# First layer: the gated rows of seven heads turned by VectorE in 32x32 blocks and through DRAM, the norm's weight applied where they are split

## The chip, the cores and the metric

The kernel runs on one core of a Trainium2 chip. The metric is device time in microseconds of one execution; times shown are medians of several runs. One more execution is taken with the hardware profiler, and all lines of the profile come from that one.

## What is computed

A decoder of two layers on 512 rows of 2048 columns, in float32. The first layer has differential attention with 8 heads (two score maps of 128 columns each, values of 256 columns); the second has another attention with 16 heads, which the change does not touch. Of the reference, cut to the first layer's part behind the attention weights:

```python
def rms_norm(x, g):
    xf = x.astype(jnp.float32)
    y = xf * lax.rsqrt(jnp.mean(jnp.square(xf), axis=-1, keepdims=True) + EPS)
    return (y * g.astype(jnp.float32)).astype(x.dtype)

def diff_attention(h, w_in, w_out, lq1, lk1, lq2, lk2, subln_g, layer_idx):
    ...
        a = p[:, :, 0] - lam * p[:, :, 1]
        return jnp.einsum('bhqk,bkhe->bqhe', a.astype(v.dtype), v)

    o = from_blocks(lax.map(block, (to_blocks(q), jnp.arange(S // BLOCK))))
    o = rms_norm(o, subln_g) * (1.0 - lam_init)
    o = o.reshape(B, S, A_WIDTH) * jax.nn.silu(g)
    return o @ w_out
```

So each head gives 512 rows of 256 columns `o`, which are normalised over their 256 columns, multiplied by the norm's weight `subln_g` (one number per column, the same for all heads), gated, and multiplied with `w_out`.

## The kernel before

TensorE (PE) multiplies in a format of fewer bits than float32, so each float32 operand is cut into a high part (a cast on ScalarE, ACT) and the remainder (a subtraction on VectorE, DVE); `split` does that, and `products` (lines 212 to 214) makes three matmuls of each product: high times high, high times low, low times high. [...]

The weights stream through four buffers `wst` of 512 KB, one per block of 256 weight rows, loaded by SyncE (SP) three blocks ahead; ACT and DVE cut each block into `whi` and `wlo` (lines 117 and 118) two blocks ahead of PE. `group` runs one set of 512 weight columns: 8 blocks, each with four bursts of six matmuls. After every burst it calls `tick`, which takes the next entry of the list `pieces` (an entry is a function, a list of functions, or nothing) and now and then a step of `background`, the sums of the modulation weights (`ms`, `macc`, line 440) that DVE makes. In this way the attention of one head is written, step by step, between the bursts of another head's projection. `drain` empties the list.

The groups run in this order: the rest of heads 0 and 1, the query and key columns of head 2 with head 0's attention beside them, the value and gate columns of head 2 with head 1's attention, and then for h = 3 to 7 the query and key columns of head h and the value and gate columns of head h with the attention of head h - 1 spread over both. Head 7's attention stands in the first group of the output projection, which follows.

`attention_a(h)` makes one head's steps. `score(i, comp)` makes a 128-row block of one score map and its exponentials in a tile `e` (four buffers). The weights of row block i must be transposed before they can be multiplied with the values. In heads 0, 1 and 7 (`turn`) PE does that through the PSUM bank `tr`, which has one buffer. In heads 2 to 6 (`spread`) `turn_small` lets DVE transpose 32x32 blocks, writes the result to DRAM (`turned`), `send` reads it back in four DMAs that put the blocks in place, and `take` cuts it into `ah` and `al` (lines 790 and 791). `values(i)` multiplies with the values; after every second i, `norm(p)` makes the gated rows `og` of two row blocks, p = 0 or 1 (128 partitions, 2 row blocks, 256 columns; one buffer): two reads of the PSUM bank on ACT (816, 817), the reciprocal root in some ten short DVE instructions, and the gate (821).

The output projection needs the gated rows transposed, columns on partitions. `store(i)` does it for one row block: two PE transposes of 128x128 into the bank `tr` (line 835) and two ACT instructions (line 837) that move them to `ogT`, with the norm's weight `subg`, a column with one number per partition, as their scale. `ogT` has 16 tiles of 128x512, two per head (e = 0 and 1 for the two halves of the 256 columns), in the pool `K` of 16 buffers. In the last projection group (`vg[7]`), `split_og` cuts them into `Hh` and `Hl`, four instructions for each head's two tiles (lines 207 and 208 as called from line 884): heads 0 to 6 there, head 7 after its attention.

The order of each engine's instructions is that in which the steps are written, as the scheduler of the framework lays them down at build time. All loads, stores and turned blocks in this part are issued by SP, in one queue; an instruction that waits there holds what is behind it. The steps that the prediction speaks of are `store` (827 to 840), the lists that `attention_a` returns (842 to 857), `split_og` (881 to 884) and the lines that put the lists into `pieces` (887 to 920).

Of the kernel before, what the change touches and what calls it, by code (L numbers as in the profile page):

```python
# [148 lines left out]
def tile_yoco(  # L149
# [23 lines left out]
    nc = tc.nc  # L173
    V, S, PE, G = nc.vector, nc.scalar, nc.tensor, nc.gpsimd
# [8 lines left out]
    kpool = ctx.enter_context(tc.tile_pool(name="kpool", bufs=16))  # L183
    wpool = ctx.enter_context(tc.tile_pool(name="wpool", bufs=2))
    ps = ctx.enter_context(tc.tile_pool(name="ps", bufs=1, space=PSUM))
    dram = ctx.enter_context(tc.tile_pool(name="dram", bufs=1, space=bass.MemoryType.DRAM))
# [19 lines left out]
    def split(hi, lo, src):  # L206
        S.copy(hi, src)
        V.tensor_tensor(lo, src, hi.bitcast(F32), op=ALU.subtract)
# [114 lines left out]
    pieces = []  # L323
# [360 lines left out]
    def evac_qk(h):  # L684
        def fn(b, acc):
            name = ("q0", "q1", "k0", "k1")[b]
            hi = ap.tile([P, T], F32R, name=name + "h", tag=name + "h")
            lo = ap.tile([P, T], F32R, name=name + "l", tag=name + "l")
            if b < 2:
                S.activation(hi, acc, AF.Copy, scale=QS)  # L690
                V.scalar_tensor_tensor(lo, acc, QS, hi.bitcast(F32), op0=ALU.mult, op1=ALU.subtract)
            else:
                split(hi, lo, acc)
            cur[h, name] = (hi, lo)
        return fn
# [16 lines left out]
    def attention_a(h, lead=3, late=(), spread=False):  # L712
# [5 lines left out]
        def score(i, comp):  # L718
            def fn():
                if i == 0 and comp == 0:  # L720
                    bias = ap.tile([P, 512], F32, name="bias", tag="bias", bufs=1)
                    V.scalar_tensor_tensor(bias, dist, -slope, mask, op0=ALU.mult, op1=ALU.add)
                    st["bias"] = bias
                if comp == 0:
                    st["mn", i] = ap.tile([P, 2], F32, name="mn", tag="mn", bufs=2)
                    st["rs", i] = ap.tile([P, 2], F32, name="rsum", tag="rsum", bufs=2)
                w = (i + 1) * P
                n = max(w, 256)
                q, k = cur[h, f"q{comp}"], cur[h, f"k{comp}"]
                sc = sc_bank()  # L730
                ts = slice(i * P, (i + 1) * P)
                products(sc[:, :n], (q[0][:, ts], q[1][:, ts]), (k[0][:, :n], k[1][:, :n]), True, True)
                e = ap.tile([P, 512], F32, name="e", tag="e", bufs=4)
                mn, rs = st["mn", i][:, comp : comp + 1], st["rs", i][:, comp : comp + 1]
                V.tensor_tensor_reduce(  # L735
                    out=e[:, :w], in0=sc[:, :w], in1=st["bias"][:, (3 - i) * P :], scale=-1.0, scalar=3.0e38,
                    op0=ALU.add, op1=ALU.min, accum_out=mn,
                )
                S.activation(e[:, :w], e[:, :w], AF.Exp, bias=mn, scale=-1.0, accum_out=rs)  # L739
                st["e", i, comp] = e  # L740
                if comp == 1:
                    rs = st["rs", i]
                    r = ap.tile([P, 2], F32, name="rrec", tag="rrec", bufs=4)
                    V.reciprocal(r, rs)
                    V.scalar_tensor_tensor(r[:, 1:2], r[:, 1:2], neglam, rs[:, 0:1], op0=ALU.mult, op1=ALU.mult)
                    e0, e1 = st["e", i, 0], e
                    V.scalar_tensor_tensor(e0[:, :w], e1[:, :w], r[:, 1:2], e0[:, :w], op0=ALU.mult, op1=ALU.add)
                    st["r", i] = r[:, 0:1]
            return fn

        def turn(i):
            def fn():
                w = (i + 1) * P
# [41 lines left out]
        def values(i):  # L795
            def fn():
                if i % 2 == 0:
                    st["o", i // 2] = o_bank()
                o = st["o", i // 2][:, (i % 2) * 256 : (i % 2 + 1) * 256]
                ah, al = st["a", i]  # L800
                vh, vl = cur[h, "v"]
                for j in range(i + 1):
                    js = slice(j * P, (j + 1) * P)
                    products(o, (ah[:, js], al[:, js]), (vh[:, j, :], vl[:, j, :]), j == 0, j == i)
                if i % 2 == 1:
                    norm(i // 2)
            return fn
# [19 lines left out]
        def store(i):  # L827
            def fn():
                if i == 0:
                    for e in range(2):  # L830
                        ogT[2 * h + e] = kpool.tile([P, T], F32, name="ogT", tag="K")
                pt = tr_bank()
                og = st["og", i // 2]
                for e in range(2):
                    PE.transpose(pt[:, e * P : (e + 1) * P], og[:, i % 2, e * P : (e + 1) * P], ident)  # L835
                for e in range(2):
                    S.activation(
                        ogT[2 * h + e][:, i * P : (i + 1) * P], pt[:, e * P : (e + 1) * P], AF.Copy, scale=subg[:, e : e + 1]
                    )
            return fn  # L840

        if spread:
            r, d, k = ([part(i) for i in range(TB)] for part in (turn_small, send, take))
            first = [
                score(0, 0), None, score(0, 1), None, [score(1, 0), r[0]], None, [score(1, 1), d[0]], None, [k[0], r[1]], None,
                [score(2, 0), d[1]], values(0), k[1], None, score(2, 1), None, [values(1), r[2]], score(3, 0), d[2], None, k[2],
                score(3, 1),
            ]
            rest = [
                values(2), r[3], store(0), d[3], store(1), k[3], None, None, None, values(3), *[None] * 9, store(2), None, store(3),  # L850
            ]
            return first, rest
        return [
            *[None] * lead, score(0, 0), *late[0:1], score(0, 1), *late[1:2], score(1, 0), *late[2:3], score(1, 1), *late[3:4],
            turn(0), score(2, 0), values(0), turn(1), score(2, 1), values(1), score(3, 0), turn(2), score(3, 1), None,
            values(2), store(0), turn(3), store(1), values(3), None, None, None, None, store(2), store(3),
        ]

    def drain():
        while pieces:  # L860
# [20 lines left out]
    def split_og(kts):  # L881
        for kt in kts:
            new_h(kt)
            split(Hh[kt], Hl[kt], ogT[kt])


    drain()
    pieces.append(lambda_columns)
    pieces.extend(attention_a(0, 2))
    group(qk[2], False, lambda b, acc: keep(("qk", b), acc), bg=lambda k: k % 3 == 2)  # L890
    drain()
    pieces.extend(first_qk(1))
    pieces.append(lambda: evac_qk(1)(3, raw["k1"]))
    pieces.extend(attention_a(1, 2, first_vg(1, part[1])))

    def keep_vg(b, acc):
        if b == 0:
# [4 lines left out]
    for h in range(3, A_HEADS):  # L902

        first_steps, rest = attention_a(h - 1, spread=True)
        if h == 3:
            pieces.extend(lambda b=b: evac_qk(2)(b, raw["qk", b]) for b in range(4))
            late = first_vg(2, raw)
            for n in range(4):
                first_steps[2 * n + 1] = late[n]
        else:  # L910
            pieces.extend([None] * 4)
        pieces.extend(first_steps)

        def evac(b, acc, h=h):
            if b == 0:
                drain()
            evac_qk(h)(b, acc)

# [12 lines left out]
        group(vg[h], True, evac_rest, bg=lambda k: k % 8 in (1, 4, 6), after_sub=early if h == A_HEADS - 1 else None)  # L931
# [549 lines left out]
```

## Time and profile before

| | us |
|---|---|
| median of 3 runs (1960.11 to 1963.65) | 1962.01 |
| the profiled execution, whole | 1961.92 |
| its span, first to last instruction | 1960.1 |
| PE busy in it | 1930.6 |
| DVE busy | 1320.9 |
| ACT busy | 708.3 |

The span is cut by the profile into instructions with a start and a duration. A line such as L835 is that of kernel.py. PE's matmuls overlap each other, so that their durations add up to more than the time they take; their starts tell how many follow each other in a stretch. "PEld" is PE's loading of the stationary operand. A name like `tr<-ident,og` gives output and inputs by the program's tile names. The number behind "idle before" or in square brackets is how long the engine stood idle ahead of the instruction, and the arrow what ended it. "SPq" is SP's queue, in which DMAs are issued.

### The profile page before, as it was taken

Reading aid. Unit: us, or ns where it says so; the run is one execution under the profiler, and the core shown is the slowest. Engines: PE = TensorE matmul, PEld = TensorE weight load, DVE = VectorE, ACT = ScalarE, POOL = GpSimd, SP = SyncE. Lnnn points to the kernel's source line nnn. Section 1 sums busy time; section 2 is a strip of 40 time slices with the busy share of each in tenths; the row PEclk is TensorE's granted clock in tenths of the full one; section 3 lists DMA queues with packets and bytes.
Section 4 is the critical chain, followed back from the end, with each engine's and each line's share of the span. In section 5 each row is a group of like instructions: output and inputs, shape, how many; then the busy total and the mean of one; then the engine's idle time right before and its main releaser. Section 6 shows DMA issues by size and latency. Waiting matters only on the chain.

```text
span 1960.1 us, 25084 instructions
## 1 busy us (share of the span) xinstructions
PE 1930.6 (98%) x8861; PEld 1600.3 (82%) x8861; DVE 1320.9 (67%) x2316; ACT 708.3 (36%) x1233; POOL 2.2 (0%) x10
## 2 busy tenths in 40 slices
PE   7999999999999999999999999999999999999997
PEld 6788888888888888888888888888888888888886
DVE  7794678877777777553475665666466666696657
ACT  3322445333333334431264222224343444453123
POOL 0000000000000000000000000000000000000000
PEclk9999999999999999999999999999999999999999
DMA  9993465777777775262345765664355555556622
GB/s 351 346 328 97 152 196 176 245 225 237 227 238 234 237 228 181 86 170 97 114 155 195 262 231 194 222 222 136 103 152 154 153 158 147 156 160 217 203 88 106
DMA packets 301018, 371.40 MB, mean 189 GB/s; under 512 B 57526, under 2 KB 220620, under 8 KB 300124
## 3 DMA queue, kind: packets, MB, share of 16 engines
q1 hardware_dynamic: 298464, 365.56, 58.3%
q10 hardware_dynamic: 2428, 4.23, 0.6%
q8 instruction: 70, 1.15, 0.2%
q14 instruction: 56, 0.46, 0.1%
HBM read 343.27 MB, written 26.43 MB: 189 GB/s over the span
## 4 chain that ended last, share of the span: by engine, by line
PE 94%; DVE 3%; DMA 2%; ACT 1%; issue 0%; SPq 0%; DVEq 0%; ACTq 0%
PE acc L212 27%; PE acc L213 26%; PE acc L214 26%; PE acc L623 3%; PE sc L625 2%; DMA sms<-in_w_mod_dram 1%; PE o L212 1%; PE sc L214 1%; PE sc L213 1%; PE o L214 1%; PE sc L212 1%; PE o L213 1%; PE o L625 1%; DVE sacc L535 1%; PE tr L835 0%
## 5 line engine op out<-in xcount | busy, mean ns | idle before, releaser
L118 DVE TENSOR_TENSOR wlo<-wst,whi 128x1024 fp32r<-128x1024 f32 (+1 forms) x290 | 350.0, 1207 | 353.9 <-ACT whi L117 344.5
L117 ACT CAST whi<-wst 128x1024 fp32r<-128x1024 f32 (+1 forms) x290 | 301.1, 1039 | 634.0 <-PE acc L214 334.6
L212 PE MATMUL acc<-hh,whi 128*128 128x512 f32 x1184 | 463.9, 392 | 0.0
L213 PE MATMUL acc<-hl,whi 128*128 128x512 f32 x1184 | 461.8, 390 | 0.0
L214 PE MATMUL acc<-hh,wlo 128*128 128x512 f32 x1184 | 461.5, 390 | 0.0
L212 PE MATMUL acc<-whi,hh 128*128 128x512 f32 x1104 | 434.6, 394 | 0.0
L214 PE MATMUL acc<-whi,hl 128*128 128x512 f32 x1104 | 430.6, 390 | 0.0
L213 PE MATMUL acc<-wlo,hh 128*128 128x512 f32 x1104 | 430.5, 390 | 0.1
L214 PEld LDWEIGHTS acc<-hh,wlo 128*128 128x128 f32 x1184 | 222.3, 188 | 47.2
L212 PEld LDWEIGHTS acc<-hh,whi 128*128 128x128 f32 x1184 | 222.6, 188 | 42.8
L213 PEld LDWEIGHTS acc<-hl,whi 128*128 128x128 f32 x1184 | 222.6, 188 | 41.9
L214 PEld LDWEIGHTS acc<-whi,hl 128*128 128x128 f32 x1104 | 207.3, 188 | 43.9
L213 PEld LDWEIGHTS acc<-wlo,hh 128*128 128x128 f32 x1104 | 207.5, 188 | 40.9 <-DVE wlo L118 0.5
L212 PEld LDWEIGHTS acc<-whi,hh 128*128 128x128 f32 x1104 | 207.4, 188 | 40.8
L440 DVE SCALAR_TENSOR_TENSOR macc<-ms,cact,macc 128x1024 f32<-128x1024 f32 (+1 forms) x180 | 198.1, 1101 | 25.5 <-DMA ms<-in_kv_w_mod_dram 13.5
L535 DVE SCALAR_TENSOR_TENSOR sacc<-sms,cact,sacc 128x512 f32<-128x512 f32 x117 | 87.8, 751 | 12.2 <-DMA sms<-in_w_mod_dram 9.3
L739 ACT ACTIVATE e<-e,mn 128x128 f32<-128x128 f32 (+3 forms) x64 | 36.0, 563 | 100.7 <-DVE mn L735 97.6
L126 ACT CAST whi<-wst 128x768 fp32r<-128x768 f32 (+1 forms) x32 | 30.1, 942 | 113.4 <-DMA wst<-in_a_w_in_dram 46.5
L1283 ACT ACTIVATE eb<-eb,mnb 128x128 f32<-128x128 f32 (+1 forms) x64 | 36.0, 563 | 86.0 <-DVE mnb L1280 85.8
L623 PE MATMUL acc<-whi,hh 128*128 128x512 f32 x128 | 51.8, 409 | 0.0
L623 PE MATMUL acc<-wlo,hh 128*128 128x512 f32 x128 | 50.6, 395 | 1.2 <-DVE wlo L135 1.2
L623 PE MATMUL acc<-whi,hl 128*128 128x512 f32 x128 | 50.7, 396 | 0.0
(273 smaller groups left out, 1996.3 us busy)
## 6 DMA issues: line engine op xcount, KB each, us to landing
wst<-in_a_w_in_dram SPq DMA_DIRECT2D x240, 256.0 KB, 3.9
ms<-in_w_mod_dram SPq DMA_DIRECT2D x64, 512.0 KB, 4.3
ms<-in_kv_w_mod_dram SPq DMA_DIRECT2D x64, 512.0 KB, 4.5
wst<-in_kv_w_dram SPq DMA_DIRECT2D x64, 512.0 KB, 3.7
sms<-in_w_mod_dram SPq DMA_DIRECT2D x56, 512.0 KB, 7.5
wst<-in_b_w_in_dram SPq DMA_DIRECT2D x112, 256.0 KB, 3.0
wst<-in_a_w_out_dram SPq DMA_DIRECT2D x32, 512.0 KB, 3.6
msk<-in_w_mod_dram SPq DMA_DIRECT2D x64, 256.0 KB, 5.3
```

What stands on the lines that cost most here:

```text
L117: self.nc.scalar.copy(hi[:, :, :w], st[:, :, :w])
L118: self.nc.vector.tensor_tensor(lo[:, :, :w], st[:, :, :w], hi[:, :, :w].bitcast(F32), op=ALU.subtract)
L126: self.nc.scalar.copy(hi[:, :, : job.width], self.stage[self.done][:, :, : job.width])
L212: PE.matmul(dst, lhs[0], rhs[0], start=start, stop=False)
L213: PE.matmul(dst, lhs[0], rhs[1], start=False, stop=False)
L214: PE.matmul(dst, lhs[1], rhs[0], start=False, stop=stop)
L440: ins = V.scalar_tensor_tensor(acc, w, cact[:, kt : kt + 1], acc, op0=ALU.mult, op1=ALU.add)
L535: V.scalar_tensor_tensor(acc, w, sc, acc, op0=ALU.mult, op1=ALU.add)
L623: PE.matmul(bank(v, b), h[:, bs], w, start=start, stop=stop)
L625: PE.matmul(bank(v, b), w[:, bs], h, start=start, stop=stop)
L739: S.activation(e[:, :w], e[:, :w], AF.Exp, bias=mn, scale=-1.0, accum_out=rs)
L1283: S.activation(e[:, :w], e[:, :w], AF.Exp, bias=mn, scale=-1.0, accum_out=rs)
```

## The change

For heads 0 to 6 the PE transposes are left out. `turn_rows(p)` lets DVE transpose the 32x32 blocks of the gated rows of two row blocks into an `e` tile, writing every fourth column, and writes this to DRAM (256 KB, a contiguous run per partition). `send_rows(p)` reads it back in four DMAs of 64 KB, in runs of 512 bytes, into a tile `ogR` of the pool `K`. The result holds, for p, the columns of the head on partitions with the two halves e and the four row sets interleaved in the free dimension: position (t, r, e) is row t of row block 2p + r, half e. `split_og` takes it apart: for each of the two tiles `Hh`, `Hl` of a head it reads half a tile from each `ogR` with a step of four elements, and applies the weight `subg` there, as ACT's scale and in DVE's instruction, which now multiplies and subtracts. Per head that is four ACT and four DVE instructions of 128x256 instead of two and two of 128x512. Head 7 keeps `store`.

In the spread heads the first write stands where `store(0)` was, one step ahead of `send(3)`; its read follows three steps later, together with `take(3)`. The second write stands where `store(2)` was, and its read three steps later. In heads 0 and 1 the last two functions of a head are given back as `rows_left` and put beside the first steps of the next head (the evictions of its queries and keys).

```diff
+        def turn_rows(p):
+            def fn():
+                t = ap.tile([P, 512], F32, name="e", tag="e", bufs=4)
+                src = st["og", p].rearrange("p r (e b c) -> p b (r e) c", e=2, b=4)
+                V.transpose(t.rearrange("p (b m n) -> p b n m", b=4, n=4), src)
+                st["turned", p] = dram.tile([P, 512], F32, name="turned_rows", tag="turned_rows", bufs=2)
+                nc.sync.dma_start(st["turned", p], t)
+            return fn
+
+        def send_rows(p):
+            def fn():
+                to = ogT[2 * h + p] = kpool.tile([P, T], F32, name="ogR", tag="K")
+                src = st["turned", p].rearrange("(a c) (b n) -> b c a n", a=4, b=4)
+                for b in range(4):
+                    nc.sync.dma_start(to[32 * b : 32 * b + 32, :].rearrange("p (a n) -> p a n", a=4), src[b])
+            return fn
...
             rest = [
-                values(2), r[3], store(0), d[3], store(1), k[3], None, None, None, values(3), *[None] * 9, store(2), None, store(3),
+                va[2], tu[3], tr[0], se[3], None, [ta[3], sr[0]], None, None, None, va[3], *[None] * 9, tr[1], None, None, sr[1],
             ]
             return first, rest
         return [
...
             turn(0), score(2, 0), values(0), turn(1), score(2, 1), values(1), score(3, 0), turn(2), score(3, 1), None,
-            values(2), store(0), turn(3), store(1), values(3), None, None, None, None, store(2), store(3),
-        ]
+            values(2), turn(3), tr[0], None, values(3), sr[0],
+        ], (tr[1], sr[1])
...
     def split_og(kts):
         for kt in kts:
             new_h(kt)
-            split(Hh[kt], Hl[kt], ogT[kt])
+            h, e = divmod(kt, 2)
+            if h == A_HEADS - 1:
+                split(Hh[kt], Hl[kt], ogT[kt])
+                continue
+            g = subg[:, e : e + 1]
+            for p in range(2):
+                src = ogT[2 * h + p].rearrange("k (t r e) -> k e r t", r=2, e=2)[:, e]
+                hi, lo = (t[kt][:, 256 * p : 256 * p + 256].rearrange("k (r t) -> k r t", r=2) for t in (Hh, Hl))
+                S.activation(hi, src, AF.Copy, scale=g)
+                V.scalar_tensor_tensor(lo, src, g, hi.bitcast(F32), op0=ALU.mult, op1=ALU.subtract)
...
-    pieces.extend(attention_a(0, 2))
+    steps, rows_left = attention_a(0, 2)
+    pieces.extend(steps)
     group(qk[2], False, lambda b, acc: keep(("qk", b), acc), bg=lambda k: k % 3 == 2)
     drain()
-    pieces.extend(first_qk(1))
-    pieces.append(lambda: evac_qk(1)(3, raw["k1"]))
-    pieces.extend(attention_a(1, 2, first_vg(1, part[1])))
+    todo = [*first_qk(1), lambda: evac_qk(1)(3, raw["k1"])]
+    todo[0], todo[2] = [todo[0], rows_left[0]], [todo[2], rows_left[1]]
+    pieces.extend(todo)
+    steps, rows_left = attention_a(1, 2, first_vg(1, part[1]))
+    pieces.extend(steps)
```

Here `tu`, `se`, `ta`, `va`, `tr` and `sr` are the lists of `turn_small`, `send`, `take`, `values`, `turn_rows` and `send_rows`; head 7 gets the list of before, written out. For head 1 the two functions left over stand in the same way beside the evictions of head 2's queries and keys.

More of the change, by code (lines that the diff above doesn't have):

```diff
@@ L840, in store @@
             return fn
+        def turn_rows(p):
[13 more added lines that the diff above has]
+            return fn
+        tu, se, ta, va, tr, sr = ([part(i) for i in range(n)] for part, n in (
+            (turn_small, 4), (send, 4), (take, 4), (values, 4), (turn_rows, 2), (send_rows, 2),
+        ))
+        if h == A_HEADS - 1:
+            return [
+                *[None] * lead, score(0, 0), score(0, 1), score(1, 0), score(1, 1),
+                turn(0), score(2, 0), values(0), turn(1), score(2, 1), values(1), score(3, 0), turn(2), score(3, 1), None,
+                values(2), store(0), turn(3), store(1), values(3), None, None, None, None, store(2), store(3),
+            ]
         if spread:
-            r, d, k = ([part(i) for i in range(TB)] for part in (turn_small, send, take))
             first = [
-                score(0, 0), None, score(0, 1), None, [score(1, 0), r[0]], None, [score(1, 1), d[0]], None, [k[0], r[1]], None,
-                [score(2, 0), d[1]], values(0), k[1], None, score(2, 1), None, [values(1), r[2]], score(3, 0), d[2], None, k[2],
+                score(0, 0), None, score(0, 1), None, [score(1, 0), tu[0]], None, [score(1, 1), se[0]], None, [ta[0], tu[1]], None,
+                [score(2, 0), se[1]], va[0], ta[1], None, score(2, 1), None, [va[1], tu[2]], score(3, 0), se[2], None, ta[2],
                 score(3, 1),
@@ L883, in split_og @@
             new_h(kt)
-            split(Hh[kt], Hl[kt], ogT[kt])
+            h, e = divmod(kt, 2)
+            if h == A_HEADS - 1:
+                split(Hh[kt], Hl[kt], ogT[kt])
[6 more added lines that the diff above has]
+                V.scalar_tensor_tensor(lo, src, g, hi.bitcast(F32), op0=ALU.mult, op1=ALU.subtract)
     drain()
     pieces.append(lambda_columns)
-    pieces.extend(attention_a(0, 2))
+    steps, rows_left = attention_a(0, 2)
+    pieces.extend(steps)
     group(qk[2], False, lambda b, acc: keep(("qk", b), acc), bg=lambda k: k % 3 == 2)
     drain()
-    pieces.extend(first_qk(1))
-    pieces.append(lambda: evac_qk(1)(3, raw["k1"]))
-    pieces.extend(attention_a(1, 2, first_vg(1, part[1])))
+    todo = [*first_qk(1), lambda: evac_qk(1)(3, raw["k1"])]
[3 more added lines that the diff above has]
+    pieces.extend(steps)
     def keep_vg(b, acc):
@@ L905, in tile_yoco @@
         if h == 3:
-            pieces.extend(lambda b=b: evac_qk(2)(b, raw["qk", b]) for b in range(4))
+            todo = [lambda b=b: evac_qk(2)(b, raw["qk", b]) for b in range(4)]
+            todo[0], todo[3] = [todo[0], rows_left[0]], [todo[3], rows_left[1]]
+            pieces.extend(todo)
             late = first_vg(2, raw)
```

## Prediction

> **What bounds the kernel now.** I read the page first: its busy times, then the chain that ended last.
>
> ```profile
> span 1960.1 us, 25084 instructions
> PE 1930.6 (98%) x8861; PEld 1600.3 (82%) x8861; DVE 1320.9 (67%) x2316; ACT 708.3 (36%) x1233; POOL 2.2 (0%) x10
> PE 94%; DVE 3%; DMA 2%; ACT 1%; issue 0%; SPq 0%; DVEq 0%; ACTq 0%
> ```
>
> TensorE (PE) is busy for 98% of the span and is 94% of the chain. A busy PE need not be a PE at its peak, so the stages come next. The change lies between 230 us (the first head's attention) and 815 us (the end of the group in which the gated rows are split). The table of stretches gives the length, then busy times of PE, weight load, VectorE (DVE), ScalarE (ACT) and POOL, granted clock, DMA share, GB/s; the last row is the sum over 230 to 815:
>
> ```profile
> 379.00:764.00 385.00, 385.00 (x1792) 320.19 (x1791) 292.42 (x505) 138.10 (x273) 0.00 (x0) 1.00 0.73 230
> 764.00:815.00 51.00, 51.00 (x242) 42.28 (x241) 28.77 (x54) 24.22 (x48) 0.00 (x0) 1.00 0.39 124
> sum 585.00, PE 584.71 PEld 485.96 DVE 439.18 ACT 233.02 POOL 0.00; mean PE 146.18 PEld 121.49 DVE 109.79 ACT 58.26 POOL 0.00
> ```
>
> PE has practically no idle time there, at the full clock. DVE is idle for 585.0 - 439.2 = 146 us, ACT for 352 us. What is taken out of PE's own queue should come off the end; work put on DVE or ACT costs nothing until PE has to wait for it.
>
> **What goes: 56 transposes on PE.** Seven heads have four stores each, of two transposes. PE's timeline around one store (start, duration), and the group's row with its mean:
>
> ```profile
> 382.34 0.39 PE L213 MATMUL acc<-wlo,hh 128*128 128x512 f32 x1
> 382.57 0.39 PE L214 MATMUL acc<-whi,hl 128*128 128x512 f32 x1
> 382.80 0.38 PE L835 MATMUL tr<-ident,og 128*128 128x128 f32 x2
> 382.94 0.48 PE L212 MATMUL acc<-whi,hh 128*128 128x512 f32 x1
> 383.25 0.39 PE L213 MATMUL acc<-wlo,hh 128*128 128x512 f32 x1
> L835 PE MATMUL tr<-ident,og 128*128 128x128 f32 x64 | 12.4, 275 | 0.3 <-DVE og L821 0.2
> ```
>
> Durations overlap, so the starts are what counts. A 512-column matmul starts 0.23 us after the one ahead of it (382.34 to 382.57). From 382.57 to 383.25 two such steps would take 0.45 us; with the pair of transposes they take 0.68. One store costs PE 0.23 us. All 28 cost 28 x 0.23 = **6.4 us**.
>
> [...]
>
> In heads 0 and 1, whose steps are not spread, three stores come before their gated rows are ready:
>
> ```profile
> 267.17 0.39 PE L214 MATMUL acc<-hh,wlo 128*128 128x512 f32 x1
> 267.66 0.41 PE L835 MATMUL tr<-ident,og 128*128 128x128 f32 x2
> 318.94 0.39 PE L213 MATMUL acc<-wlo,hh 128*128 128x512 f32 x1
> 319.24 0.41 PE L835 MATMUL tr<-ident,og 128*128 128x128 f32 x2
> 330.36 0.39 PE L213 MATMUL acc<-hl,whi 128*128 128x512 f32 x1
> 330.93 0.44 PE L835 MATMUL tr<-ident,og 128*128 128x128 f32 x2 [0.18 <-DVE og L821]
> ```
>
> The steps are 0.49, 0.30 and 0.57 us where 0.23 is normal: 0.26 + 0.07 + 0.34 = **0.7 us** of waiting, which goes too. What is late next there is DVE's turning of the same rows, and no matmul reads these before the output projection.
>
> **What comes on DVE and ACT.** The nearest rows (the two og rows stand for the new split: half as wide, with a scale from a column):
>
> ```profile
> L837 ACT ACTIVATE ogT<-tr,subg 128x128 f32<-128x128 f32 x64 | 20.0, 363 | 51.3 <-PE tr L835 51.3
> L207 ACT CAST hh<-ogT 128x512 fp32r<-128x512 f32 x16 | 9.9, 620 | 13.8 <-PE acc L213 13.4
> L208 DVE TENSOR_TENSOR hl<-ogT,hh 128x512 fp32r<-128x512 f32 x16 | 10.9, 692 | 15.6 <-ACT hh L207 9.6 <-PE acc L213 6.0
> L816 ACT ACTIVATE og<-o,rrec 128x256 f32<-128x256 f32 x32 | 15.2, 475 | 21.5 <-PE o L214 21.0
> L821 DVE SCALAR_TENSOR_TENSOR og<-og,rstd,sg 128x256 f32<-128x256 f32 x32 | 14.1, 482 | 0.4
> L1294 DVE STREAM_TRANSPOSE tb<-eb 128x512 f32<-128x512 f32 x16 | 11.3, 708 | 0.3
> ```
>
> ACT loses 56 x 0.363 = 20.3 us of evictions (and their waits for PE), and gains 14 x (2 x 0.475 - 0.620) = 4.6 us in the split. DVE gains 14 x 0.708 = 9.9 us of turning and 14 x (2 x 0.482 - 0.692) = 3.8 us in the split: 13.7 us against 146 idle. The turning writes, and the split reads, every fourth element, which no row shows. Below, no gain is possible from that; above, I take twice the row: 1.4 us a turning, so 13.7 becomes 13.7 + 9.9 + 14 x 0.96 = 37 us, still under 146. So I cost all of it at nothing. The cover is DVE's idle time; in 764 to 815, where six of the seven heads are split, it is 51.0 - 28.8 = 22 us, and the splits' 3.3 (at worst 15) fit. If DVE had no cover, 13.7 us would come on top.
>
> **What comes on the queue of SP.** Fourteen writes of 256 KB and 56 reads of 64 KB, like those with which heads 2 to 6 already turn their last block:
>
> ```profile
> turned<-e SPq DMA_DIRECT2D x5, 256.0 KB, 3.1
> e<-turned SPq DMA_DIRECT2D x20, 64.0 KB, 3.5
> 482.65 1.75 SPq L780 DMA_DIRECT2D e<-turned  x4
> DMA to landing us min/median/max: 1.8/2.9/5.3
> SPq L780 <- DMA turned<-e: 25.6, 19, 2.7
> ACT whi L117 <- DMA wst<-in_a_w_in_dram: 4.4, 1, 4.4
> ```
>
> Four reads are issued in 1.75 us (third row; the fourth is the landing of these blocks' writes and reads), so the 70 take about 31 us of SP's 585; POOL's queue has no part in it. A write waits for its turning, a read for the landing of its write; meanwhile the weight (wst) and modulation (ms) loads behind it stand. The write is placed three steps or more of 1.4 us ahead of its read, about the landing of 3.1 us; SP's longest such wait now is 2.7 us (fifth row). Weights are loaded three blocks ahead, and their cast waited for a load once in the window (last row). Bounds: 0 to 14 x 2.7 = 38 us on SP; on PE I take nothing, since each wait alone is shorter than one block's 24 matmuls (24 x 0.23 = 5.4 us).
>
> **Where a wait comes on PE.** In heads 2 to 6 the first row write goes out between the write of the last turned block and that block's read, which values(3) needs. That place is tight already. ACT's cast and PE's products for head 2; the cast for heads 3 and 4, and head 4's reads; DVE's remainder and the PE product that needs it for heads 5 and 6:
>
> ```profile
> 392.26 0.62 ACT L790 CAST ah<-e 128x512 fp32r<-128x512 f32 x1 [0.88 <-DMA e<-turned]
> 393.27 0.40 PE L212 MATMUL acc<-whi,hh 128*128 128x512 f32 x1
> 393.66 0.39 PE L214 MATMUL o<-vh,al 128*128 128x256 f32 x1
> 487.94 0.61 ACT L790 CAST ah<-e 128x512 fp32r<-128x512 f32 x1
> 579.30 1.95 SPq L780 DMA_DIRECT2D e<-turned  x4
> 584.21 0.61 ACT L790 CAST ah<-e 128x512 fp32r<-128x512 f32 x1
> 679.01 0.69 DVE L791 TENSOR_TENSOR al<-e,ah 128x512 fp32r<-128x512 f32 x1 [1.64 <-ACT ah L790]
> 682.30 0.28 PE L214 MATMUL o<-vh,al 128*128 128x256 f32 x1
> 776.09 0.69 DVE L791 TENSOR_TENSOR al<-e,ah 128x512 fp32r<-128x512 f32 x1
> 778.49 0.28 PE L214 MATMUL o<-vh,al 128*128 128x256 f32 x1
> ```
>
> In head 2 the cast waits for the DMA and PE for the cast (a step of 0.39). PE now comes 2 x 0.23 = 0.46 us sooner, so that head waits 0.46 + D, where D is how much later the read lands. In heads 3 and 4 the cast shows no DMA wait; their reads were out at 484.40 (482.65 + 1.75) and 581.25, 3.54 and 2.96 us ahead of it. Landing takes 1.8 us at the least, so the slack lies between 0 and 1.7, and 0 and 1.2; I take about the middles, 0.9 and 0.6. Heads 5 and 6 have 682.30 - 679.70 = 2.6 and 778.49 - 776.78 = 1.7 us. D lies between 0 and 3.1 us (the whole landing of a 256 KB write). The write is issued some 2 us ahead of the read and mostly done by then, so I take D = 0.5: waits of 0.96 + 0.06 + 0.36 + 0 + 0 = **1.4 us**. Behind the waiting cast stand ACT's weight casts, which PE needs only two blocks later.
>
> **Sum:** -6.4 - 0.7 + 1.4 = -5.7 us. The profiled execution took 1961.92 us (its span and 1.8 us around it), the median of the runs is 1962.01, so one sum serves both: **1956.2 us**.
>
> **Rivals.** (a) *The whole durations go*, 15.4 instead of 6.4: 1961.9 - 15.4 - 0.7 + 1.4 = 1947.2. The starts speak against it: 0.03. (b) *The wait for values(3) takes the gain.* With D = 2 the five heads wait 2.5 + 1.6 + 1.9 + 0 + 0.8 = 6.8 us, about the 7.1 that goes: 1961.6. For it speaks that head 2 waits already and DMA is 73% busy; against it, that the reads come after most of the row write: 0.15. (c) *The same place, slower.* Were the read to stand behind the whole landing of the row write, D = 3.1: 3.6 + 2.7 + 3.0 + 1.0 + 1.9 = 12.2 us, 1961.9 - 7.1 + 12.2 = 1967.0. From D = 2.9 on (11 us of waits) the change is slower by more than 0.2%. It would need SP or DVE to hold the row write until the read is due: 0.08.
>
> **Chances and range.** The forecast, D up to 1.1, has 0.74. A measurement of this kernel can tell about 0.2%, 3.9 us, from no change. Faster by more than that: 0.74 + 0.03 = 0.77; within: 0.15; slower: 0.08. The forecast's bounds are 1961.9 - 7.1 = 1954.8 (no wait) and 1958.1; the range reaches half a microsecond below the first and over more than half of (b), 1954.0 to 1960.3, and leaves out (a), (c) and the rest of (b).
>
> **What would show it.** Line 835's transposes fall from 64 to 8 and their steps of 0.68 us vanish between 255 and 797 us; PE stays busy without idle rows. Two turnings of some 0.7 us appear in each of seven heads, splits of 128x256 after 764 us. The step on D is judged by PE's step ahead of the product with al in values(3), heads 2 to 6. I am wrong if PE waits there for several microseconds, if weight casts begin to wait for wst loads, or if PE's steps elsewhere grow.

## The result, and the profile after

| | us |
|---|---|
| before, median of 6 runs (1960.11 to 1963.65) | 1961.56 |
| after, median of 6 runs (1953.48 to 1955.85) | 1954.73 |
| after / before | 0.9965, 95% interval 0.9955 to 0.9975 |
| the profiled execution of after, whole | 1955.55 |
| its span | 1953.8 |

The change is faster by 0.35%. The two profiled executions lie 1961.92 - 1955.55 = 6.4 us apart; the forecast was 5.7. The page of after, first its busy times, then the chain that ended last:

```profile
span 1953.8 us, 25057 instructions
PE 1924.2 (98%) x8805; PEld 1595.6 (82%) x8805; DVE 1339.7 (69%) x2344; ACT 702.4 (36%) x1191; POOL 2.2 (0%) x10
PE 92%; DMA 4%; DVE 3%; SPq 1%; issue 1%; ACT 0%; DVEq 0%
```

PE is what it was, the bound, with 8861 - 8805 = 56 matmuls fewer. The table of stretches of after over the same times as before (length, busy PE, PEld, DVE, ACT, POOL, clock, DMA share, GB/s), and its sum over 230 to 815:

```profile
330.00:379.00 49.00, 48.46 (x227) 40.26 (x226) 41.98 (x85) 18.86 (x39) 0.00 (x0) 1.00 0.78 240
379.00:764.00 385.00, 384.96 (x1775) 319.65 (x1775) 300.02 (x517) 129.75 (x242) 0.00 (x0) 1.00 0.78 243
764.00:815.00 51.00, 51.00 (x238) 42.65 (x237) 37.87 (x78) 33.51 (x60) 0.00 (x0) 1.00 0.45 140
sum 585.00, PE 584.42 PEld 486.44 DVE 460.84 ACT 229.25 POOL 0.00; mean PE 146.11 PEld 121.61 DVE 115.21 ACT 57.31 POOL 0.00
```

DVE has 21.7 us more in this window (460.84 against 439.18), and PE is still busy without a break except for half a microsecond between 330 and 379. The groups of the new instructions in after:

```profile
L846 DVE STREAM_TRANSPOSE e<-og 128x512 f32<-128x512 f32 x14 | 15.4, 1098 | 0.0
L917 ACT ACTIVATE hh<-ogR,subg 128x256 fp32r<-128x256 f32 x28 | 19.6, 750 | 13.7 <-PE acc L213 13.7
L918 DVE SCALAR_TENSOR_TENSOR hl<-ogR,subg,hh 128x256 fp32r<-128x256 f32 x28 | 18.4, 672 | 7.2 <-ACT hh L917 7.2
```

The turning takes 1.10 us (0.708 was taken from the dense row), the split 0.750 on ACT and 0.672 on DVE (0.475 and 0.482 taken). Each is 39 to 58% more than the row it was taken from; the turning stays inside its bound of 1.4 us. Whether the step of four elements makes the difference is looked at with e6.

To see where the 6.4 us come from, the same instruction is looked up in both traces. DVE's first instruction on head 0's scores opens the stretch of the change, and its first gate of the output projection comes just after it. Before, then after (start, duration):

```profile
227.20 0.29 DVE L735 CUSTOM_DVE_ANT_0 e<-sc,bias 128x128 f32<-128x128 f32 x1 [3.29 <-PE sc L214]
860.66 0.68 DVE L979 TENSOR_TENSOR ztmp<-acc,gate 128x512 f32<-128x512 f32 x1
```

```profile
226.26 0.29 DVE L735 CUSTOM_DVE_ANT_0 e<-sc,bias 128x128 f32<-128x128 f32 x1 [3.29 <-PE sc L214]
853.57 0.68 DVE L1018 TENSOR_TENSOR ztmp<-acc,gate 128x512 f32<-128x512 f32 x1
```

After is 0.94 us ahead before the change has done anything, and 7.09 ahead at the end: the stretch became **6.15 us** shorter. All kernels below are read in this way. "Ahead" is the shift against before at the stretch's start, "stretch" what the stretch gained or lost, "1004" the change of the shift around 1004 us, where the last normalised rows go through DRAM (further down); negative is earlier or shorter.

| kernel | median us (runs) | ratio, interval | ahead | stretch | 1004 |
|---|---|---|---|---|---|
| after | 1954.73 (6) | 0.9965, 0.9955 to 0.9975 | -0.9 | -6.2 | +0.6 |
| after, run once more (e9) | 1954.42 (5) | 0.9962, 0.9948 to 0.9975 | -0.9 | -6.2 | +1.1 |
| e1, before without the transposes | 1955.85 (8) | 0.9972, 0.9961 to 0.9982 | -1.6 | -6.5 | +1.1 |
| e2, after with the transposes back | 1963.29 (11) | 1.0011, 1.0002 to 1.0020 | -1.3 | +1.6 | 0.0 |
| e3, after without DVE's turning | 1955.06 (5) | 0.9965, 0.9951 to 0.9979 | -0.4 | -7.5 | +0.8 |
| e4, turning held at its written place | 1958.55 (9) | 0.9986, 0.9977 to 0.9995 | -2.0 | -3.7 | +0.6 |
| e5, after without the way through DRAM | 1956.15 (8) | 0.9973, 0.9962 to 0.9983 | -2.1 | -6.1 | +0.6 |
| e6, turning written without gaps | 1953.84 (5) | 0.9962, 0.9949 to 0.9974 | -0.6 | -8.3 | +0.9 |
| e7, after with 24 small matmuls at the start | 1953.73 (5) | 0.9962, 0.9950 to 0.9975 | -1.5 | -8.3 | 0.0 |
| e8, e6 and e7 together | 1954.93 (5) | 0.9965, 0.9953 to 0.9978 | +0.9 | -7.6 | 0.0 |
| e10, before with the 24 small matmuls | 1963.20 (11) | 1.0005, 0.9997 to 1.0014 | -2.1 | +0.9 | 0.0 |

The column "ahead" covers work that is the same in all of them (but for the small matmuls) and spreads over 3 us. So a total from one execution says nothing on a microsecond; the stretch by itself says more, since e9 repeats after's to 0.04 us, though before's own stretch moved by 0.9 in e10. Of e4's eleven executions two took 4766 and 10203 us, where the other nine lie between 1957 and 1961; its median is that of the nine.

### The profile page after: what moved, and what is told of

Read it like the earlier page. It is cut to its first block, busy times and chain, and to the rows that moved or that the text cites. A ratio compares the mean times of both kernels' runs of the same rounds, so it can differ in the third digit from the quotient of the medians.

```text
span 1953.8 us, 25057 instructions
## 1 busy us (share of the span) xinstructions
PE 1924.2 (98%) x8805; PEld 1595.6 (82%) x8805; DVE 1339.7 (69%) x2344; ACT 702.4 (36%) x1191; POOL 2.2 (0%) x10
## 3 DMA queue, kind: packets, MB, share of 16 engines
q8 instruction: 69, 1.13, 0.2%
## 4 chain that ended last, share of the span: by engine, by line
PE 92%; DMA 4%; DVE 3%; SPq 1%; issue 1%; ACT 0%; DVEq 0%
PE acc L212 26%; PE acc L213 26%; PE acc L214 26%; PE acc L623 3%; PE sc L625 2%; DMA sms<-in_w_mod_dram 1%; PE o L212 1%; DMA ms<-in_w_mod_dram 1%; PE o L214 1%; PE o L213 1%; PE sc L214 1%; PE sc L213 1%; PE sc L212 1%; PE o L625 1%; DVE sacc L535 1%
```

## The experiments

### e1: the transposes alone are taken out of before

In before, heads 0 to 6 no longer transpose; ACT's two instructions read the gated rows straight from `og`. This leaves the turning out of the computation. ACT's moves to `ogT` remain.

```diff
-                pt = tr_bank()
                 og = st["og", i // 2]
+                if h == A_HEADS - 1:
+                    pt = tr_bank()
+                    for e in range(2):
+                        PE.transpose(pt[:, e * P : (e + 1) * P], og[:, i % 2, e * P : (e + 1) * P], ident)
                 for e in range(2):
-                    PE.transpose(pt[:, e * P : (e + 1) * P], og[:, i % 2, e * P : (e + 1) * P], ident)
-                for e in range(2):
-                    S.activation(
-                        ogT[2 * h + e][:, i * P : (i + 1) * P], pt[:, e * P : (e + 1) * P], AF.Copy, scale=subg[:, e : e + 1]
-                    )
+                    src = pt[:, e * P : (e + 1) * P] if h == A_HEADS - 1 else og[:, i % 2, e * P : (e + 1) * P]
+                    S.activation(ogT[2 * h + e][:, i * P : (i + 1) * P], src, AF.Copy, scale=subg[:, e : e + 1])
```

> The kernel before with the 56 PE transposes of heads 0 to 6 left out: ACT's 56 evictions read the gated rows as they are, so the rows are not turned (that part of the computation is missing). Nothing else is added. Theory PE (PE's queue sets the end, a store costs it 0.23 us): 6.4 us less than before, and the 0.7 us of early stores in heads 0 and 1 as well, about 7.1 less, 1954.5. Rival ACT (the gain comes from ACT, which no longer evicts): ACT still has all its evictions, so no gain, 1961.5. Rival duration (each transpose is worth its 0.275 us): 15.4 less, 1946.

The stretch gained 6.5 us, as much as with the whole change, though ACT kept its 56 instructions. It would be more but for 1.0 us of waits of PE that e1 has and before has not: 0.6 for a cast ahead of the values, 0.4 for the gate columns. The group of e1 that shows ACT's instructions:

```profile
L839 ACT ACTIVATE ogT<-og,subg 128x128 f32<-128x128 f32 x56 | 18.3, 393 | 35.0 <-DVE og L821 35.0
```

The gain is PE's time, not ACT's relief.

### e2: the transposes are put back into after

Two transposes per row block into the bank `tr`, which nobody reads, at the places that `store` had (in heads 0 and 1 close to them); all of the new path stays.

```diff
+        def extra(i):
+            def fn():
+                pt = tr_bank()
+                og = st["og", i // 2]
+                for e in range(2):
+                    PE.transpose(pt[:, e * P : (e + 1) * P], og[:, i % 2, e * P : (e + 1) * P], ident)
+            return fn
...
-                va[2], tu[3], tr[0], se[3], None, [ta[3], sr[0]], None, None, None, va[3], *[None] * 9, tr[1], None, None, sr[1],
+                va[2], tu[3], [extra(0), tr[0]], se[3], extra(1), [ta[3], sr[0]], None, None, None, va[3], *[None] * 9, [extra(2), tr[1]], None, extra(3), sr[1],
```

> The changed kernel with the 56 PE transposes put back at their old steps, their result unread: ACT has no evictions, DVE and DMA turn the rows as in the change. Theory PE: 28 x 0.23 = 6.4 us more than the changed kernel, 1961. Rival ACT: no change against the changed kernel, 1954.7. Rival duration: 15.4 more, 1970.

The whole gain is gone: 1963.29, and a stretch 1.57 - (-6.15) = 7.7 us longer than after's. The starts said 28 x 0.23 = 6.4 for the transposes themselves. The summary of PE's waits in e2 over the stretch (in total, times, longest) has 0.9 us, a transpose that waits for its gated rows again among them:

```profile
PE o L212 <- ACT ah L790: 0.4, 1, 0.4
PE tr L856 <- DVE og L821: 0.3, 1, 0.3
PE acc L212 <- DVE k1l L208: 0.2, 1, 0.2
```

After has 0.5 us of such waits itself, so close to a microsecond of the 7.7 stays without a name. e1 and e2 together, the one taking out and the other putting back, give 6.5 and 7.7 us for the 28 pairs with the waits that come and go; a price by whole durations (15.4) is out. The new path by itself, e2 against before, costs between nothing and 0.2%.

### e3, e5, e6: the parts of the new path

e3 sends `og` to DRAM without DVE's turning, which is thus left out of the result. e5 lets DVE turn into the tile of the split and leaves out the 14 writes and 56 reads, so that the blocks are not put in their places. e6 keeps all of the computation but writes the turning without gaps, and the split reads runs of 32 with 56 smaller instructions on each engine.

```diff
 e3
-                t = ap.tile([P, 512], F32, name="e", tag="e", bufs=4)
-                src = st["og", p].rearrange("p r (e b c) -> p b (r e) c", e=2, b=4)
-                V.transpose(t.rearrange("p (b m n) -> p b n m", b=4, n=4), src)
+                t = st["og", p].rearrange("p r n -> p (r n)")
 e5
-                t = ap.tile([P, 512], F32, name="e", tag="e", bufs=4)
+                t = ogT[2 * h + p] = kpool.tile([P, T], F32, name="ogR", tag="K")
...
-                nc.sync.dma_start(st["turned", p], t)
 e6
-                V.transpose(t.rearrange("p (b m n) -> p b n m", b=4, n=4), src)
+                V.transpose(t.rearrange("p (b n m) -> p b n m", b=4, n=4), src)
...
+                for r in range(2):
+                    src = ogT[2 * h + p].rearrange("k (a r e m) -> k r e a m", a=4, r=2, e=2)[:, r, e]
+                    ts = slice(256 * p + 128 * r, 256 * p + 128 * r + 128)
+                    hi, lo = (t[kt][:, ts].rearrange("k (a m) -> k a m", a=4) for t in (Hh, Hl))
```

> The changed kernel without DVE's 14 turnings: the gated rows go to DRAM as they are, so the rows are not turned within the blocks (that part of the computation is missing). Looked at: PE's wait of 0.7 us for q0l at the start of head 3's value group (374 us). Theory DVE (two turnings of 1.1 us stand ahead of the remainder that frees PE's bank): this wait goes, 0.7 to 0.8 us less up to 430 us. Rival DMA (row writes and reads make the loads of modulation weights late, and DVE waits for these): the wait stays, since all DMAs are still there. In total 0.7 to 1.2 us less than the changed kernel, about 1954, or the same.

> The changed kernel without the way through DRAM: DVE turns the rows into the tile that is split, the 14 writes and 56 reads are left out (so the blocks stay where they are; that part of the computation is missing). Theory: DVE, not DMA, makes the 0.7 us of PE's wait at 374 us, so that one stays; the waits of PE for the remainder in values (0.27 us at 349 us, 0.56 us at 581 us) are due to the landing of turned blocks and become smaller. Up to 860 us some 0.5 us less than the changed kernel. Rival: the row DMAs on SP's queue cost PE several microseconds, and as many go.

> The changed kernel with DVE's turning written in contiguous runs of 32 columns and the split taking those runs (four ACT and four DVE instructions of 128x128 for each tile of a head, not two and two of 128x256 at a step of four elements). The same result. Theory: a turning takes 0.71 us again (before: 0.708 for a contiguous 128x512) and not 1.10, so two of them give 0.8 us back ahead of q0l, and PE's wait of 0.7 us at 374 us all but goes; some 0.7 us less than the changed kernel, 1954.0. The split: 4 x 0.36 us against 2 x 0.75 on ACT, the same. Rival (1.1 us of the turning is DVE's own cost of a 32x32 block order, not of the step in its writes): 1.1 us stays, and so does the wait.

No median is measurably below after's. So neither the 15.4 us of turning on DVE nor the 70 DMAs cost what their own size would say. The groups of e6:

```profile
L846 DVE STREAM_TRANSPOSE e<-og 128x512 f32<-128x512 f32 x14 | 9.9, 705 | 0.0
L919 ACT ACTIVATE hh<-ogR,subg 128x128 fp32r<-128x128 f32 x56 | 18.0, 391 | 15.0 <-PE acc L213 15.0
```

The same operation, dense, takes 0.705 us, the figure of the prediction; the 0.39 us more in after (1.098 us, +56%) are the price of the gaps alone. Why writing at a step of four float32 costs that much, no run shows; only this step and none were compared. For the split not even the step is shown to be the cause. Its +58% and +39% are against rows of other instructions (ACT's reads PSUM), and in e6, with runs of 32, ACT needs 2 x 0.391 us for what takes 0.750 in after.

In the stretches, e3 (-7.5) and e6 (-8.3) gain 1.3 and 2.2 us more than after. e5 (-6.1) does not, but it lost 0.8 us at 348.90 where values wait for a cast, and 0.4 for the gate columns, much as e1 did; after has neither as a listed wait:

```profile
348.90 0.39 PE L212 MATMUL o<-vh,ah 128*128 128x256 f32 x1 [0.81 <-ACT ah L790]
```

### Where after loses a part: 374 us

PE's only listed wait in after's stretch, and what DVE did ahead of it (DVE's timeline, with the idle time before an instruction and what ended it):

```profile
374.86 0.50 PE L212 MATMUL acc<-whi,hh 128*128 128x512 f32 x1 [0.54 <-DVE q0l L691]
360.62 1.28 DVE L440 SCALAR_TENSOR_TENSOR macc<-ms,cact,macc 128x1024 f32<-128x1024 f32 x1 [0.41 <-DMA ms<-in_w_mod_dram]
363.25 1.28 DVE L440 SCALAR_TENSOR_TENSOR macc<-ms,cact,macc 128x1024 f32<-128x1024 f32 x1 [0.51 <-DMA ms<-in_w_mod_dram]
368.66 1.12 DVE L846 STREAM_TRANSPOSE e<-og 128x512 f32<-128x512 f32 x1
374.13 0.68 DVE L691 SCALAR_TENSOR_TENSOR q0l<-acc,q0h 128x512 fp32r<-128x512 f32 x1
```

PE waits for the PSUM bank that DVE's remainder of head 3's queries (691) must free. From 363.25 on DVE runs without a gap, the new turning among it. After, run once more (e9), has the same wait, larger, and behind a longer wait of DVE for a modulation load:

```profile
363.69 1.28 DVE L440 SCALAR_TENSOR_TENSOR macc<-ms,cact,macc 128x1024 f32<-128x1024 f32 x1 [1.60 <-DMA ms<-in_w_mod_dram]
375.30 0.50 PE L212 MATMUL acc<-whi,hh 128*128 128x512 f32 x1 [1.08 <-DVE q0l L691]
```

e7 has the same instructions here, its turning with 1.10 us too, but no wait for a load just ahead of them and none of PE. Between 340 and 376 us DVE waits 2.0 and 2.2 us for such loads in the two executions of after, 0.2 in e7, and with a shorter or no turning 1.0 (e6), 0.4 (e8) and 0.2 (e3); PE has the wait in the first two alone. e5, whose expectation was that this wait stays, turns in 1.09 us at the same place, waits for no load there, and PE's wait is gone. So the turning by itself does not make the wait.

It takes room, though. In before, without a turning, the remainder ends 1.5 us before PE needs the bank (375.47 + 0.68 to 377.62), in e7, with one, 0.5 us (372.14 + 0.68 to 373.34). In the last 15 us ahead of the remainder DVE waits for loads 0.9 us in after and 1.6 in e9, more than what the turning leaves. This fits all the executions; no run held the loads back on purpose, so it is not shown by itself.

### e4: the turning held at its written place

The trace of after showed that DVE's first turning of heads 2 to 6 stands far ahead of its place in the list. In head 2 it starts at 368.66, just behind the gate that makes its rows, and the turning of the last block, behind which it is written, at 380.69. So the order of an engine's instructions is not always that in which the steps are written, as the description of the kernel has it: the build put this one 12 us ahead of the turning behind which it is written. Head 2 on SP's queue in after:

```profile
376.37 0.46 SPq L848 DMA_DIRECT2D turned_rows<-e  x1
381.43 0.33 SPq L772 DMA_DIRECT2D turned<-e  x1
384.59 1.75 SPq L780 DMA_DIRECT2D e<-turned  x4
386.39 1.97 SPq L856 DMA_DIRECT2D ogR<-turned_rows  x4
```

The row write (848) goes out 5 us ahead of the last turned block's write (772), not between that and its read (780), as the prediction had it. e4 pins it:

```diff
-                V.transpose(t.rearrange("p (b m n) -> p b n m", b=4, n=4), src)
+                tc.keep_in_program_order(V.transpose(t.rearrange("p (b m n) -> p b n m", b=4, n=4), src))
```

> The changed kernel with DVE's turning pinned where its step is written, behind the turning of the last block, and not some 18 us ahead of it, where the build puts it. Now the row write does go out between the write of the last turned block and its read, as the prediction had it. Theory DVE for the 0.7 us at 374 us: the turning of head 2 is no longer ahead of the bank's remainder and the wait goes. The prediction's D (0.5 us later landing): waits in values(3) of heads 2 to 6 add up to about 1.4 us, so in total -0.7 + 0.8 = the same as the changed kernel within 0.5 us. If D is the whole landing of 3 us: 12 us of waits, over 1965. If D is nothing: 0.7 to 1.2 us less.

Now the order is the predicted one. SP and ACT in e4, head 2:

```profile
378.51 0.34 SPq L772 DMA_DIRECT2D turned<-e  x1
380.71 0.33 SPq L848 DMA_DIRECT2D turned_rows<-e  x1
382.51 1.75 SPq L780 DMA_DIRECT2D e<-turned  x4
386.42 0.62 ACT L790 CAST ah<-e 128x512 fp32r<-128x512 f32 x1 [0.24 <-DMA e<-turned]
```

The cast waits 0.24 us for the read, less than the 0.88 of before, and PE has no wait over 0.15 us at values(3) of any head. So D, the delay of that read, is about nothing even in the order that was feared.

In after, the measure that the prediction named, PE's step ahead of the product with al, is 0.23, 0.25, 0.39, 0.26 and 0.12 us in heads 2 to 6 (before: 0.39, 0.23, 0.23, 0.12 and 0.12). Head 4 waits now, where head 2 waited before, each some 0.4 us with the steps around it; in e9 it is head 2 again. ACT and PE for head 4 in after:

```profile
579.97 0.62 ACT L790 CAST ah<-e 128x512 fp32r<-128x512 f32 x1 [0.95 <-DMA e<-turned]
581.37 0.39 PE L214 MATMUL o<-vh,al 128*128 128x256 f32 x1
```

Why this read lands late, with no row write between the block's write and its read, stays open.

Yet e4 is 3.8 us slower than after by the medians and 2.4 by the stretch, which none of the cases in its expectation had. The loss is elsewhere: PE, DVE and SP in e4 where PE goes on from head 4's value and gate columns to head 5's queries:

```profile
515.35 0.47 PE L212 MATMUL acc<-hh,whi 128*128 128x512 f32 x1 [0.44 <-DVE sg L709]
511.58 1.28 DVE L440 SCALAR_TENSOR_TENSOR macc<-ms,cact,macc 128x1024 f32<-128x1024 f32 x1 [3.15 <-DMA ms<-in_kv_w_mod_dram]
505.69 1.75 SPq L856 DMA_DIRECT2D ogR<-turned_rows  x4
507.54 0.85 SPq L425 DMA_DIRECT2D ms<-in_kv_w_mod_dram  x2
PE acc L212 <- DVE sg L709: 3.1, 4, 1.1
```

Read from below: SP issues the row reads for 1.75 us, and behind them the modulation loads. DVE waits 3.15 us for one of these, comes late to the gate columns (709), and PE waits for the bank that they hold. PE waits so four times, 3.1 us in all (last row, the summary of PE's waits): twice here and twice around 708 us, between heads 6 and 7, where DVE waits 5.2 us for a load. SP has its own part in it: its row reads wait 18.8 us for the landing of their writes in e4 and 6.8 in after, and what is behind them waits along. So the row DMAs can have a price on PE, by way of the modulation loads, once they stand in a bad place in SP's queue. This chain is read from e4's trace; no run took the reads alone from that place.

### e7 to e10: what is given back at 1004 us

Far behind the change, after loses 0.6 us of what it had. The last normalised rows go to DRAM and come back; DVE's next copy waits for that write, and PE for the copy. DVE and PE in after:

```profile
1004.80 1.29 DVE L1089 COPY n<-sc 128x512 f32<-128x512 f32 x2 [0.52 <-DMA n_dram<-n]
1005.54 0.66 PE L1076 MATMUL sc<-ident,n 128*128 128x128 f32 x4 [0.52 <-DVE n L1089]
```

The change touches none of this. The view of the DMAs from the issue of this write on, in 40 slices of 0.15 us, of after and then of before:

```profile
GB/s 0 0 0 0 0 0 819 55 819 55 765 55 765 109 710 109 819 109 655 164 546 273 55 0 0 0 0 55 0 55 0 55 0 55 0 0 0 0 0 0
q8 instruction: 1, 0.02, 1.0%
```

```profile
GB/s 0 0 0 0 0 0 819 55 819 55 819 55 765 109 765 109 765 109 710 164 601 273 0 0 0 0 0 0 0 0 0 0 0 0 0 0 0 0 0 0
```

In after a packet of instructions falls into the write. It takes 1.0% of 16 engines' 6.0 us, which is 0.96 us of one engine, and the write has a tail that before's has not: single slices of 55 GB/s, one packet of 8 KB in every second slice, the last of them 12 slices, about 1.8 us, behind the end of before's. That this tail is the share of the one engine that has the packet is the author's reading; the view does not tell the engines apart. The page of after has 69 such packets of 16 KB (q8 instruction, 1.13 MB), one for 255 of PE's 8805 matmuls and as many weight loads. Whose instructions they hold the page does not say. If they are PE's, as the author takes them to be, which write is hit depends on how many PE instructions come before it, and the change takes 56 matmuls and their weight loads out. e7 puts 24 one-column matmuls at the very start, which nobody reads (48 matmul records and as many weight loads), to move these packets without changing anything else:

```diff
+    pt = tr_bank()
+    for j in range(24):
+        PE.matmul(pt[:, j : j + 1], ident, ident[:, 0:1], start=True, stop=True)
```

> The changed kernel with 24 one-column matmuls in the first 6 us, where PE waits for the first loads: 48 more instructions in PE's stream. Looked at: the 0.6 us given back at 1005 us, where DVE's copy waits for the last write of the normalised rows. Theory fetch: a 16 KB packet of PE's instruction stream, one per some 256 instructions, falls into that write (1001.4 us) and holds the end of it on one DMA engine; 48 instructions earlier it falls some 5 us earlier, ahead of the write, and the wait of 0.5 us on DVE and of 0.68 us on PE goes, 0.6 us less from 998 to 1098 us. Rival (the write is late because the stage comes earlier): it stays at 0.6 us. The matmuls themselves: up to 1 us at the start, nothing after it.

In e7 no instruction packet falls into the write, and the loss is 0.0. DVE's copy and PE there:

```profile
1001.54 1.28 DVE L1092 COPY n<-sc 128x512 f32<-128x512 f32 x2
1002.28 0.66 PE L1079 MATMUL sc<-ident,n 128*128 128x128 f32 x4
```

Then e6 and e7 together, after once more, and before with the same matmuls:

> The turning written without gaps (as in e6) together with the 48 extra PE instructions of one column each at the start (as in e7). If the fetch of PE instructions inside the last write of the normalised rows costs the 0.6 to 1.0 us near 1000 us, and if the turning's gaps cost the rest, this kernel has neither: no PE wait over 0.2 us between 230 and 870 us, none over 0.2 us between 995 and 1010 us, a shift against before of -8.3 us or more at the first eviction of the output projection that is kept to the end, and a median 0.7 to 1.0 us below e6's (1952.9 us, ratio about 0.9957). If the two gains of e6 and e7 are differences between single executions only, the median stays at e6's and e7's 1953.8 us.

> The changed kernel a second time, nothing altered. Its PE instruction stream is the same, so the fetch theory expects the packet of instructions inside the last write of the normalised rows again, and PE's wait of 0.5 to 1.0 us near 1005 us again. If that wait is a matter of one execution, it is gone. The wait of 0.7 us at 374 us is open: if it belongs to the turning's 1.1 us it is there again; if it belongs to when transfers landed in that one execution it moves or goes. Median 1954.7 us +- 0.7, ratio 0.9965.

> The kernel before with the same 48 extra PE instructions at the start. Before has no fetch inside the last write of the normalised rows, so the fetch theory expects nothing from moving the fetches: the median of before plus at most 0.1 us (ratio 0.9995 to 1.001). If the extra instructions themselves shorten something at the start, as e7's 1 us below the changed kernel could also be read, before would become about 1 us faster with them (ratio 0.9995 or below).

The traces agree with the fetch theory. The same view of this write has one instruction packet in after, e9, e1 and e3, which lose 0.6 to 1.1 us here, and none in before, e2, e7 and e8, which lose nothing. Of e4, e5 and e6, which lose 0.6, 0.6 and 0.9 us, and of e10, which loses nothing, no such view is shown. In e9:

```profile
1006.07 0.65 PE L1076 MATMUL sc<-ident,n 128*128 128x128 f32 x4 [0.94 <-DVE n L1089]
```

The times say less. e8 has the wait neither at 374 nor at 1004 us, but its median is 1954.93 where 1952.9 was expected, PE has a wait of 0.4 us at the values of a head where none over 0.2 was expected, and its shift at the end of the stretch is -6.7 us, not -8.3: that expectation failed. e8's profiled execution came 0.9 us late to the stretch where after came 0.9 early, and the medians of after, e6, e7, e8 and e9 lie within 1.2 us with intervals of about 2 us each way. No version here is shown to beat after. In e10 the small matmuls gain nothing on before (1.0005, 0.9997 to 1.0014); its median is higher by 1.7 us, but the interval of the ratio includes 1.

## Why the prediction held, step by step

**What goes on PE, 6.4 us: right.** 56 matmuls went; taking them out alone gave 6.5 us, 1.0 of new waits against it (e1), putting them back cost 7.7 with waits (e2). Reading the price from the starts of the neighbours and not from the 275 ns of the row (56 x 0.275 = 15.4 us) was what decided; the rival of 15.4 us is refuted.

**Waits at three early stores, 0.7 us: right in kind.** They are gone in after, and one of 0.3 us on a gated row came back in e2. The stretches without new waits (e6, e7) gained 8.3 us, about a microsecond more than the 7.1 that was to go. Part of it is head 2's old wait at values(3), some 0.4 us, which the prediction let stay; the rest is in steps too small to name, and no larger than what before's stretch moves by itself (0.9).

**DVE and ACT, at nothing: nearly.** The turning was mis-sized (1.10 for 0.708), within the bound given. The cover was read as a sum, 146 us idle; at 374 us it is not there, for DVE runs without a gap for 11 us, and PE waits 0.5 and 1.1 us in the two executions. A sum of idle time over 585 us says nothing on the one place where a bank must be freed.

**SP's queue, at nothing on PE: right for after, not as a rule.** Leaving out all 70 DMAs gained nothing measurable (e5). But e4 shows a way to PE that the step left out: it named the modulation loads behind the same reads, and then weighed only the weight loads, which are three blocks ahead.

**The wait at values(3), 1.4 us: failed.** The step that failed is "in heads 2 to 6 the first row write goes out between the write of the last turned block and that block's read". The build places the turning, and so the write, 5 to 12 us ahead of the last block's write; and where it is held at that place (e4), D is still about nothing, not 0.5. What PE waits at values(3) in after is some 0.4 us in one head, as in before, and not 1.4 more. So the rivals (b) and (c), which are larger D, had no ground either.

The sum came out (5.7 forecast, 6.2 in the stretch and 6.4 in the execution) because waits of about the predicted size arose in other places, at 374 us and a few smaller ones: a right total with a wrong term, and in this part luck. The give-back at 1004 us was in no step, nor was the 0.9 us that the execution had ahead before the change began.

## What to carry to other kernels

Price an instruction in a full PE queue by the starts of its neighbours with and without it, and take it out alone to check. When work goes to an engine with spare time, look for the places where that engine holds a PSUM bank or waits for a load, not at its total. Where a build may move instructions up, the written order is not the queue's order: look for the new DMAs in the trace before arguing about what stands behind them.

## What was not expected of the hardware

Written at a step of four float32, a DVE transpose of 128x512 took 1.098 us instead of 0.705 (after against e6, the same operation dense). Where one of after's 69 instruction packets of 16 KB fell into a write of 1 MB, the write ended about 1.8 us later than in before, and PE waited 0.52 us (0.94 in e9). e7's 24 small matmuls at the start, which change nothing else, left that write without a packet and PE without the wait, a millisecond behind them. That such packets are PE's instructions is the author's reading of these runs.
